# Group norm factors of the first three batches formed for 88 partitions by 6 numbers and spread over the channels through DRAM

## The chip, the core and the metric

The kernel runs on one core of one Trainium2 chip. The metric is the device time of one execution in microseconds, lower is better; the time of a kernel is the median of its runs. TensorE (PE) multiplies matrices into PSUM, VectorE (DVE), ScalarE (ACT) and GpSimd (POOL) work on tiles in SBUF and PSUM, SyncE (SP) issues most of the DMA transfers. Each engine takes its instructions in the order in which they were put at compile time and waits where one isn't ready.

## What is computed

One layer of a decoder for a prompt of 256 tokens and 8 sampled tokens (264 columns in all): a gated feed-forward network, a mixer that runs 16 attention heads beside 16 heads of an RWKV-7 recurrence, an output projection, and a second feed-forward network. The change lies in the group norm behind the recurrence. For every head (64 channels) and every token the 64 values are normalised:

```python
    S, y = wkv_scan(wkv0, r, logw, k, v, kk, a)
    mean = jnp.mean(y, axis=-1, keepdims=True)
    var = jnp.mean((y - mean) ** 2, axis=-1, keepdims=True)
    yn = ((y - mean) * lax.rsqrt(var + GN_EPS)).reshape(B, T, RWKV_WIDTH) * ln_w.astype(f32) + ln_b.astype(f32)
    bonus = jnp.sum(r * k * r_k.astype(f32), axis=-1, keepdims=True) * v
    out = (yn + bonus.reshape(B, T, RWKV_WIDTH)) * g
```

## The kernel before

Activations lie with channels on the 128 partitions and the 264 tokens along the columns, so a pair of heads fills one tile of 128 x 264. The 16 RWKV heads are eight such pairs, worked on in four batches of two pairs.

The bulk of the time is `gemm` (line 135): weights stream from DRAM in chunks of 128 x 512 (`chunk`, line 123). SP loads a chunk into `raw` (6 buffers), ACT rounds it to `hi`, DVE takes the rest `lo` = `raw` - `hi` (4 buffers each), and PE runs twelve matmuls of 264 columns per chunk: `hi` twice, `lo` once for each of four 128 x 128 blocks. Two feed-forward networks stand around the mixer. In the mixer the input projection (`win`, 38 tiles of four chunks) and the output projection (`wout`) run as the steady stream, and the recurrence, the attention and the norm are generators ("tasks") that `tick` moves on by one step after each chunk; `pause(n)` lets a task sleep for n ticks. What the program writes in this order is then put into a fixed order on each engine by a scheduler that works with a model of the chip. So an edit in one task can move the instructions of others.

A batch goes through `prep` (gates, decay, key norm) and `chain`: a triangular solve on DVE (60 small instructions on the tiles `X`, `Xt`, `st`, ending in `PT`), a row of small PE steps (`PT`x`gm`, `TT`x`W`, `kr`x`TT`, ...) with copies on ACT and DVE between them, the states `S`, the output `y`, and last `gnorm` for each of the two pairs. `gnorm` (line 707) runs in float32 on PE: one product of `y` with a 128 x 128 matrix `cm` takes the mean away, ACT squares the result into `r`, one product with `bo` (ones within each head) sums the squares over a head's 64 channels and puts the sum on all 64 partitions, ACT takes the root, DVE the reciprocal of 128 x 264 numbers, and DVE multiplies. Behind it lines 694 and 695 apply weight, bias and gate. The product with `cm` stays in its PSUM bank (`m`, 5 buffers) until the last multiplication.

DMA transfers of the mixer go through SP too: `sa`, which carries the solve's input through DRAM to a layout with another partition order, the loads `ld` (6 buffers), the residual `x` from `xsp`. ACT issues a few output transfers, one of them `out_sh` (line 887), which waits for a copy that POOL makes.

Of the kernel before, what the change touches and what calls it, by code (L numbers as in the profile page):

```python
# [7 lines left out]
F32 = mybir.dt.float32  # L8
F32R = mybir.dt.float32r
AF = mybir.ActivationFunctionType  # L10
ALU = mybir.AluOpType
AX = mybir.AxisListType

P = 128
NP = 256
NB = 8
T = NP + NB
# [7 lines left out]
HALF = (slice(0, 64), slice(64, 128))  # L25
# [5 lines left out]
ROW = 320  # L31
NWARM = 11
NGM, NKR, NUV, NTT, NBT = 10, 5, 3, 2, 5
NSTEP = 4
DWAIT = (11, 11, 11, 3)
PW = (2, 1, 3, 2, 9)
# [1 line left out]
LKV = 26  # L38
SEQ = [('b', 0), ('b', 1), ('b', 2), ('b', 3), ('kv', 0), ('kv', 1), ('kv', 2), ('kv', 3), ('q', 0), ('q', 1), ('q', 2), ('q', 3), ('q', 4), ('q', 5), ('q', 6), ('q', 7)]
PASS = [[0,1,2,3],[4,5,6,7],[8,9,10,11,12,13,14,15]]  # L40

VG1, VGM, VG2, VGF = 0, 16, 32, 48
VMU, VKK, VKA, VA0, VRK, VLW, VLB, VSK, VSD = 64, 90, 98, 106, 114, 122, 130, 138, 154
NVEC = 155
# [3 lines left out]
def body(tc, I, O):  # L48
    nc = tc.nc
    V, A, G, TE, SP = nc.vector, nc.scalar, nc.gpsimd, nc.tensor, nc.sync  # L50
# [3 lines left out]
    def uid(s):  # L54
        cnt[0] += 1
        return f"{s}{cnt[0]}"

    def tt(e, out, a, b, op):
        return e.tensor_tensor(out=out, in0=a, in1=b, op=op)  # L59
# [8 lines left out]
    def act(out, in_, f, **k):  # L68
        return A.activation(out=out, in_=in_, func=f, **k)  # L69

    def bc(ap, shape):
        return ap.broadcast_to(list(shape))

    def mm(out, lhsT, rhs, start=True, stop=True, **k):
        return TE.matmul(out, lhsT, rhs, start=start, stop=stop, **k)  # L75

    def behind(i):
        tc.add_manual_dep(i.ins, big[0].ins.name, mybir.DependencyInfo(mybir.DependencyClass.NoSync, mybir.DependencyReason.SCHED_ONLY))
        return i
# [16 lines left out]
    def pause(n):  # L96
        for _ in range(n):
            yield

    with ExitStack() as ctx:  # L100
# [4 lines left out]
        dp = ctx.enter_context(tc.tile_pool(name="dp", bufs=1, space=bass.MemoryType.DRAM))  # L105
# [16 lines left out]
        def mp():  # L122
            return pp.tile([P, 512], F32, tag="m", bufs=NM, name=uid("m"))
# [33 lines left out]
        eps = cp.tile([P, 2], F32, name="eps")  # L157
# [199 lines left out]
        def mixing_body(mx, n2, n3, XD, XR):  # L357
# [3 lines left out]
            def ring(shape, tag, bufs):  # L361
                return mx.tile(list(shape), F32, tag=tag, bufs=bufs, name=uid(tag))
# [6 lines left out]
            ident, bo, cm = C[:, CID:CID + P], C[:, CBO:CBO + P], C[:, CCM:CCM + P]  # L369
# [50 lines left out]
            class Batch:  # L420
                pass

            def c4(x):
                return x[:, :NP].rearrange("p (c t) -> p c t", c=4)

# [127 lines left out]
            def chain(bt):  # L553
                n = bt.n
# [31 lines left out]
                for h in range(2):  # L586
                    x = h * 64
                    V.transpose(TT[x:x + 32, :, 0:32], TN[x:x + 32])
                yield from pause(7)
                ps = mp()  # L590
                for k in range(n):
                    for c in range(4):
# [14 lines left out]
                for h in range(2):  # L607
                    r = slice(h * 64, h * 64 + 32)
                    A.copy(TT[r, :, 32:64], ps[r, :n * P].rearrange("p (c t) -> p c t", t=32))
                yield  # L610
                Ys = [yb[bt.p0 + k] for k in range(n)]
                uv = bt.UV
                N = ring((P, n, 4, 64), "N", 1)
# [9 lines left out]
                for k in range(n):  # L623
                    v = wus[k].rearrange("p (c t) -> p c t", c=4)
                    for h in range(2):
                        (V.tensor_copy, A.copy)[h](uv[HALF[h], :, k, HALF[h]], v[HALF[h], :, 64:128])
                yield
                pbs = [mp() for _ in range(n)]
                for k in range(n):
                    for c in range(1, 4):  # L630
# [51 lines left out]
                    A.dma_start(O["wkvp"][bt.p0 + k], S[:, k])  # L682
                g2s = [load(I["g2"][bt.p0 + k], (P, P)) for k in range(n)]
                gps = []
                gs = [gnorm(Ys[k]) for k in range(n)]
                for _ in range(PW[3] + 1):
                    for g in gs:
                        next(g)
                    yield
# [14 lines left out]
                        A.copy(XR[HALF[h], 4], xt[0:64, HALF[h]])  # L704
                yield

            def gnorm(y):
                yp = mp()
                mm(yp[:, :T], cm, y)
                r = tmp()  # L710
                act(r, yp[:, :T], AF.Square)
                yield from pause(PW[3])
                vp = mp()
                mm(vp[:, :T], bo, r)
                act(r, vp[:, :T], AF.Sqrt, scale=1.0 / 64, bias=eps[:, 1:2])
                V.reciprocal(r, r)
                tt(V, y, yp[:, :T], r, ALU.mult)
                yield
# [395 lines left out]
```

## Time and profile before

| | |
|---|---|
| median of 3 runs | 1958.44 us (1957.58 to 1960.91) |
| the profiled execution: its own time | 1958.83 us |
| its span, first to last instruction | 1957.0 us |
| granted TensorE clock | 0.998 |
| PE busy | 1940.1 us |
| DVE busy | 1313.1 us |
| ACT busy | 1036.4 us |
| first and last product of `y` with `cm` | 904.7 and 1087.9 us |

The first feed-forward network runs up to about 780 us, the mixer from there to about 1200 us, the second network behind it. In the profile's rows a float32 matmul of the program appears as two records, each with a weight load of its own; a matmul of the gemm (float32r) is one record. Records overlap, so a mean duration is longer than the step from one to the next.

### The profile page before, as it was taken

What the parts mean: (1) busy time and instruction counts of PE and PEld (TensorE: products, weight loads), DVE (VectorE), ACT (ScalarE), POOL (GpSimd) and SP (SyncE); (2) the same over time, 40 slices, a digit from 0 to 9 for tenths busy, and PEclk for the clock granted to TensorE, in tenths of its full rate; (3) what the DMA queues carried; (4) which work ended last, traced back from release to release, by engine and by line L of the source; (5) the groups of instructions that cost most, each with busy time, mean ns of one, the idle gap of its engine ahead of it and who ended that gap; (6) DMA issues with size and microseconds to landing.
All of it is one profiled execution on the core that took longest, in us unless ns stands there. A gap on an engine that the chain in (4) does not pass through costs nothing.

```text
span 1957.0 us, 45229 instructions
## 1 busy us (share of the span) xinstructions
PE 1940.1 (99%) x17011; PEld 1922.1 (98%) x17011; DVE 1313.1 (67%) x2591; ACT 1036.4 (53%) x2069; POOL 264.1 (13%) x382
## 2 busy tenths in 40 slices
PE   9999999999999999999999999999999999999998
PEld 9999999999999999999889999999999999999998
DVE  5865555655556567799988766766666666666665
ACT  5644444444444456665556755654444444444445
POOL 0401001010010122232210000210101001010012
PEclk9999999999999999999999999999999999999999
DMA  7666666666656567555455455566666666666654
GB/s 241 178 194 194 186 194 196 184 189 178 188 183 185 184 194 230 165 162 153 136 151 167 137 157 185 176 187 188 191 189 193 188 194 191 191 195 183 195 182 148
DMA packets 218875, 357.26 MB, mean 183 GB/s; under 512 B 33552, under 2 KB 72352, under 8 KB 218656
## 3 DMA queue, kind: packets, MB, share of 16 engines
q1 hardware_dynamic: 212144, 345.76, 59.4%
q10 hardware_dynamic: 6512, 8.61, 1.4%
q8 instruction: 133, 2.18, 0.4%
q14 instruction: 86, 0.70, 0.1%
HBM read 346.67 MB, written 9.69 MB: 182 GB/s over the span
## 4 chain that ended last, share of the span: by engine, by line
PE 95%; DVE 3%; DMA 1%; issue 1%; ACT 1%; SPq 0%; DVEq 0%; POOL 0%; ACTq 0%
PE acc L75 87%; PE m L75 7%; DVE lo L59 1%; DVE Xt L59 0%; DVE st L59 0%; DMA Xt<-sa 0%; DMA x<-in_x 0%; DMA raw<-in_win 0%; DVE y L59 0%; SPq L564 0%; DVE gm L59 0%; ACT t L69 0%; DMA sa<-gm 0%; PE m L782 0%; ACT BT L521 0%
## 5 line engine op out<-in xcount | busy, mean ns | idle before, releaser
L59 DVE TENSOR_TENSOR lo<-raw,hi 128x512 fp32r<-128x512 f32 (+1 forms) x1288 | 874.5, 683 | 511.0 <-ACT hi L132 489.8
L132 ACT CAST hi<-raw 128x512 fp32r<-128x512 f32 (+1 forms) x1288 | 777.0, 606 | 822.0 <-PE acc L75 741.5
L75 PE MATMUL acc<-x,hi 128*128 128x264 f32 x5034 | 932.7, 286 | 2.2 <-DVE o L62 1.2
L75 PEld LDWEIGHTS acc<-x,hi 128*128 128x128 f32 x5034 | 781.4, 189 | 5.8 <-ACT hi L132 2.4
L75 PE MATMUL acc<-x,lo 128*128 128x264 f32 x2517 | 719.8, 286 | 0.5 <-DVE lo L59 0.5
L75 PE MATMUL acc<-h,hi 128*128 128x264 f32 x2752 | 495.0, 284 | 0.0
L75 PEld LDWEIGHTS acc<-x,lo 128*128 128x128 f32 x2517 | 475.5, 189 | 2.9 <-DVE lo L59 1.3
L75 PEld LDWEIGHTS acc<-h,hi 128*128 128x128 f32 x2752 | 424.4, 189 | 0.0
L75 PE MATMUL acc<-h,lo 128*128 128x264 f32 x1376 | 387.8, 284 | 0.0
L75 PEld LDWEIGHTS acc<-h,lo 128*128 128x128 f32 x1376 | 259.2, 189 | 0.0
L59 POOL TENSOR_TENSOR t<-t,t 128x264 f32<-128x264 f32 x74 | 80.3, 1085 | 1095.9 <-DVE t L59 949.7
L75 PE MATMUL acc<-y,hi 128*128 128x264 f32 x648 | 122.7, 284 | 0.0
L75 PE MATMUL acc<-o,hi 128*128 128x264 f32 x648 | 120.1, 284 | 0.0
L75 PE MATMUL acc<-kv,hi 128*128 128x264 f32 x582 | 109.2, 284 | 0.0
L75 PEld LDWEIGHTS acc<-y,hi 128*128 128x128 f32 x648 | 101.2, 189 | 0.1
L75 PEld LDWEIGHTS acc<-o,hi 128*128 128x128 f32 x648 | 100.1, 189 | 0.0
L62 DVE SCALAR_TENSOR_TENSOR x<-acc,x 128x264 f32<-128x264 f32 x192 | 81.2, 427 | 24.5 <-PE acc L75 23.6
L75 PE MATMUL acc<-y,lo 128*128 128x264 f32 x324 | 92.0, 284 | 0.0
L75 PE MATMUL acc<-o,lo 128*128 128x264 f32 x324 | 92.0, 284 | 0.0
L75 PEld LDWEIGHTS acc<-kv,hi 128*128 128x128 f32 x582 | 90.0, 189 | 0.0
L59 DVE TENSOR_TENSOR t<-acc,t 128x264 f32<-128x264 f32 x156 | 67.4, 432 | 32.8 <-PE acc L75 32.8
L75 PE MATMUL acc<-kv,lo 128*128 128x264 f32 x291 | 82.7, 284 | 0.0
(280 smaller groups left out, 1534.9 us busy)
## 6 DMA issues: line engine op xcount, KB each, us to landing
raw<-in_gu SPq DMA_DIRECT2D x688, 256.0 KB, 3.4
raw<-in_dn SPq DMA_DIRECT2D x224, 256.0 KB, 2.9
raw<-in_win SPq DMA_DIRECT2D x152, 256.0 KB, 3.4
raw<-in_dn SPq DMA_DIRECT2D x160, 192.0 KB, 2.7
raw<-in_wout SPq DMA_DIRECT2D x64, 256.0 KB, 3.3
xsp<-x ACTq DMA_DIRECT2D x16, 132.0 KB, 3.6
x<-xsp SPq DMA_DIRECT2D x16, 132.0 KB, 4.0
ld<-in_sT SPq DMA_DIRECT2D x16, 128.0 KB, 3.7
```

The lines of the kernel that those rows point to most:

```text
L59: return e.tensor_tensor(out=out, in0=a, in1=b, op=op)
L62: return V.scalar_tensor_tensor(out=out, in0=a, scalar=s, in1=b, op0=op0, op1=op1)
L75: return TE.matmul(out, lhsT, rhs, start=start, stop=stop, **k)
L132: A.copy(hi[:, :w], raw[:, :w])
```

## The change

For batches 0, 1 and 2 (`SMALL = (1, 1, 1, 0)`) the product with `bo` gives way to `sums`: for j = 0, 1, 2 the squares of every third token (88 columns) are the stationary operand and two columns of `bo`, one per head, the moving one. The result is 88 partitions x 6 numbers, one sum of squares for each head and token. Root and reciprocal are taken of these 6 columns. `spread` writes them to DRAM as two rows of 264 and, two ticks later, loads each row into the 64 partitions of its head, into the tile `r`; three ticks later DVE multiplies. The centred `y` is copied from PSUM to SBUF by ACT right behind the square. The generator of such a batch gets five more ticks. Batch 3 keeps the former way. `LAG`, `P1` and `P2` replace constants by names with the same values.

```diff
+LAG = (7, 7, 7, 7)
+P1 = 1
+P2 = 1
+SMALL = (1, 1, 1, 0)
+HOP = (2, 3)
...
+            def sums(sq):
+                sm = mp()
+                for j in range(3):
+                    mm(sm[0:88, j * 2:j * 2 + 2], sq[:, j:T:3], bo[:, 0:P:64])
+                return sm[0:88, 0:6].rearrange("p (j h) -> p h j", h=2)
+
+            def spread(s, to):
+                d = dp.tile([2, T], F32, tag=uid("dr"), name=uid("dr"))
+                SP.dma_start(d.rearrange("h (p j) -> p h j", j=3), s)
+                yield from pause(HOP[0])
+                for h in range(2):
+                    behind(SP.dma_start(to[HALF[h]], bc(d[h:h + 1], (64, T))))
+                yield from pause(HOP[1])
...
-                gs = [gnorm(Ys[k]) for k in range(n)]
-                for _ in range(PW[3] + 1):
+                gs = [gnorm(Ys[k], SMALL[bt.i]) for k in range(n)]
+                for _ in range(PW[3] + 1 + SMALL[bt.i] * sum(HOP)):
...
-            def gnorm(y):
+            def gnorm(y, small):
                 yp = mp()
                 mm(yp[:, :T], cm, y)
                 r = tmp()
                 act(r, yp[:, :T], AF.Square)
+                if small:
+                    A.copy(y, yp[:, :T])
+                    yield from pause(PW[3])
+                    s = ring((88, 2, 3), "s", 4)
+                    act(s, sums(r), AF.Sqrt, scale=1.0 / 64, bias=eps[0:88, 1:2])
+                    V.reciprocal(s, s)
+                    yield from spread(s, r)
+                    tt(V, y, y, r, ALU.mult)
+                    yield
+                    return
                 yield from pause(PW[3])
```

The scheduler moves much else with it, from the first norm (904.7 us) on. Three places in the order of the instructions follow. In a row, the left name is what is written, and numbers behind names are buffers.

DVE, the norm of batch 0, before (`t_12822` and `t_12826` are the two pairs' roots, `lo` the gemm's weights, `Xt` and `st` the solve of batch 1):

```order
L716 RECIPROCAL t_12822<-t_12822 128x264
L59 TENSOR_TENSOR st_13013<-X_12413,Xt_12414 128x72
L716 RECIPROCAL t_12826<-t_12826 128x264
L59 TENSOR_TENSOR lo_13221<-raw_13219,hi_13220 128x512
L59 TENSOR_TENSOR y_112<-m_12820,t_12822 128x264
L59 TENSOR_TENSOR Xt_12414<-Xt_12414,st_13013 128x4x18
L59 TENSOR_TENSOR lo_13267<-raw_13265,hi_13266 128x512
L59 TENSOR_TENSOR y_112<-m_12824,t_12826 128x264
```

and now:

```order
L735 RECIPROCAL s_12866<-s_12866 88x6
L63 TENSOR_TENSOR Xt_12414<-Xt_12414,st_12998 128x3x19
L63 TENSOR_TENSOR st_13019<-X_12413,Xt_12414 128x72
L735 RECIPROCAL s_12875<-s_12875 88x6
L63 TENSOR_TENSOR Xt_12414<-Xt_12414,st_13019 128x4x18
L63 TENSOR_TENSOR st_13022<-X_12413,Xt_12414 128x68
L63 TENSOR_TENSOR Xt_12414<-Xt_12414,st_13022 128x4x17
L63 TENSOR_TENSOR st_13025<-X_12413,Xt_12414 128x64
L63 TENSOR_TENSOR Xt_12414<-Xt_12414,st_13025 128x4x16
L462 TENSOR_SCALAR t_13035<-keep,t_12962 128x256
L63 TENSOR_TENSOR st_13028<-X_12413,Xt_12414 128x60
L63 TENSOR_TENSOR lo_13237<-raw_13235,hi_13236 128x512
```

The first multiplication of `y` stands six rows further on, behind another `lo`, and with it a wait for DMA. From the first of these reciprocals to the end of batch 1's solve (`PT`) DVE has 85 instructions with 17 `lo` before, 81 with 14 `lo` now; on PE, from batch 0's sums of squares to the first product with that `PT`, 218 matmuls of the gemm stand before, 167 now, and the other matmuls between are the same but for the sums.

SP at the same place before (`raw` are the gemm's weights, `ld` the mixer's loads):

```order
L131 DMA raw_13479<-in_win 128x512
L366 DMA ld_13297<-in_sT 128x256
L366 DMA ld_13464<-in_lw 128x256
L131 DMA raw_13516<-in_win 128x512
L131 DMA raw_13564<-in_win 128x512
```

and now:

```order
L135 DMA raw_13495<-in_win 128x512
L435 DMA dr_12873<-s_12866 88x2x3
L435 DMA dr_12882<-s_12875 88x2x3
L370 DMA ld_13313<-in_sT 128x256
L438 DMA t_12822<-dr_12873 64x264 x2
L438 DMA t_12827<-dr_12882 64x264
L135 DMA raw_13532<-in_win 128x512
L438 DMA t_12827<-dr_12882 64x264
L135 DMA raw_13580<-in_win 128x512
```

Two stores and three of the four loads stand ahead of the next weights. Counted along each engine's order, 620 chunks of the gemm stand on PE ahead of batch 0's sums, 630 on SP ahead of the first store, and 624 `lo` on DVE ahead of its first small reciprocal.

ACT, batch 1's chain, before (`TT` at line 609 is waited for by PE, `hi` are the gemm's weights):

```order
L600 COPY W_13184<-m_13497 32x256 x2
L132 COPY hi_14036<-raw_14035 128x512
L132 COPY hi_14077<-raw_14076 128x512
L887 DMA out_sh<-shc 128x234
L609 COPY TT_12420<-m_13534 32x8x32 x2
L132 COPY hi_14118<-raw_14117 128x512
L132 COPY hi_14172<-raw_14171 128x512
L622 COPY W_13184<-m_13583 128x192
```

and now, first around `TT`, then where `out_sh` stands, with nine rows left out between the two:

```order
L136 COPY hi_13942<-raw_13941 128x512
L627 COPY TT_12420<-m_13550 32x8x32 x2
L136 COPY hi_13979<-raw_13978 128x512
L136 COPY hi_14028<-raw_14027 128x512
L640 COPY W_13200<-m_13599 128x192
```

```order
L658 COPY PT_13201<-m_13655 128x192
L495 COPY uv_12919<-m_13732 64x2x64 x4
L136 COPY hi_14099<-raw_14098 128x512
L915 DMA out_sh<-shc 128x234
L136 COPY hi_14142<-raw_14141 128x512
```

The output transfer no longer stands ahead of `TT`; it is now behind `W`, `uv` and `PT` of the same batch.

More of the change, by code (lines that the diff above doesn't have):

```diff
@@ L588, in chain @@
                     V.transpose(TT[x:x + 32, :, 0:32], TN[x:x + 32])
-                yield from pause(7)
+                yield from pause(LAG[bt.i])
                 ps = mp()
@@ L609, in chain @@
                     A.copy(TT[r, :, 32:64], ps[r, :n * P].rearrange("p (c t) -> p c t", t=32))
-                yield
+                yield from pause(P1)
                 Ys = [yb[bt.p0 + k] for k in range(n)]
@@ L626, in chain @@
                         (V.tensor_copy, A.copy)[h](uv[HALF[h], :, k, HALF[h]], v[HALF[h], :, 64:128])
-                yield
+                yield from pause(P2)
                 pbs = [mp() for _ in range(n)]
```

## The prediction

> **What bounds the kernel now.** I read the page's first two parts, then the chain of waits, then who PE waited for in the stretch that the change reaches.
>
> ```profile
> PE 1940.1 (99%) x17011; PEld 1922.1 (98%) x17011; DVE 1313.1 (67%) x2591; ACT 1036.4 (53%) x2069; POOL 264.1 (13%) x382
> DVE  5865555655556567799988766766666666666665
> PE 95%; DVE 3%; DMA 1%; issue 1%; ACT 1%; SPq 0%; DVEq 0%; POOL 0%; ACTq 0%
> ```
>
> PE is busy 99% of the span and makes 95% of the chain that ended last. Time can go only where PE does less work or stands less. DVE is close to full only in the slices of the mixer (7 to 9 tenths), where the change lies. The product of `y` with `cm`, up to which both kernels have the same order on PE, is at 904.7 us; from just behind it to the end of the chains (1110 us) PE waited for:
>
> ```profile
> PE m L75 <- ACT TT L609: 1.5, 1, 1.5
> PE m L75 <- DVE W L622: 1.3, 2, 0.9
> PE acc L75 <- DVE o L62: 1.2, 1, 1.2
> PE m L701 <- ACT XR L703: 0.4, 1, 0.4
> PE m L732 <- ACT XD L536: 0.3, 1, 0.3
> PE acc L75 <- DVE lo L59: 0.3, 1, 0.3
> PE acc L75 <- DVE x L59: 0.2, 1, 0.2
> ```
>
> Columns: total us, times, longest. That is 5.2 us in all, and the most that a lighter DVE or ACT can give back.
>
> **PE's own work: nearly nothing.** Six matmuls with `bo` go, six times three with 88 x 2 results come.
>
> ```profile
> 904.87 1.05 PE L75 MATMUL m<-y,C 128*128 128x264 f32 x4
> 905.88 0.40 PE L75 MATMUL acc<-x,hi 128*128 128x264 f32 x2
> ...
> 1946.13 0.63 PE L75 MATMUL m<-ones,sq 128*88 128x1 f32 x6 [0.65 <-ACT sq L69]
> 1946.62 0.80 PE L75 MATMUL m<-sq,ones 128*128 128x128 f32 x5
> ...
> 920.77 11.81 PE acc L75 x98
> ```
>
> The last row gives a gemm matmul 11.81 / 98 = 0.12 us. Two float32 matmuls of 264 columns (four records from 904.87 on) and one gemm matmul lie ahead of 905.88, so one costs (1.01 - 0.12) / 2 = 0.45 us. The final norm at the kernel's end already forms sums in the new shape with one column: six records (three matmuls) from 1946.13 to 1946.62, 0.49 us. So 6 x (0.49 - 0.45) = +0.2 us. New is that every third column is loaded as weights; no row has that. Bounds: the smallest float32 records, and the whole duration of a weight load as if none overlapped:
>
> ```profile
> L75 PE MATMUL m<-XD,ld 64*64 64x2 f32 x256 | 8.6, 195 | 0.0
> L75 PEld LDWEIGHTS acc<-x,hi 128*128 128x128 f32 x5034 | 781.4, 189 | 5.8 <-ACT hi L132 2.4
> ```
>
> 8.6 / 256 = 0.034 us a record gives 6 x (0.20 - 0.45) = -1.5 us; 0.189 us gives 6 x (1.13 - 0.45) = +4.1 us. I take +0.2, since the final norm's matmul is the same but for the step and one column.
>
> **DVE's relief.** The large reciprocals are the dearest single instructions there:
>
> ```profile
> L716 DVE RECIPROCAL t<-t 128x264 f32<-128x264 f32 x6 | 10.7, 1798 | 1.9 <-ACT t L69 1.9
> L753 DVE RECIPROCAL stb<-stb 128x4 f32<-128x4 f32 x8 | 1.3, 169 | 0.1
> 991.68 1.80 DVE L442 RECIPROCAL t<-m 128x264 f32<-128x264 f32 x1
> 995.33 0.39 DVE L62 SCALAR_TENSOR_TENSOR o<-acc,rs 128x264 f32<-128x264 f32 x1
> 995.98 0.67 DVE L59 TENSOR_TENSOR lo<-raw,hi 128x512 fp32r<-128x512 f32 x1
> 995.86 0.36 PE L75 MATMUL acc<-x,hi 128*128 128x264 f32 x1 [1.24 <-DVE o L62]
> ```
>
> The first row's six (batches 0 to 2) shrink to the second row's size: 10.7 - 6 x 0.17 = 9.7 us of DVE, 3.2 per batch. The other rows show what a late DVE costs: a reciprocal of 1.8 us and a backlog behind it let `o` empty its bank late, and PE stands 1.2 us. In the new order batch 1's large reciprocals (3.6 us) no longer stand ahead of this, so I count the 1.2 as gone, and `W`'s 1.3 too: it waits for a copy in the same backlog. The early copy of `y` also frees a PSUM bank sooner; no wait for a bank `m` is among PE's rows, so that is worth nothing here. Multiplying from SBUF rather than from PSUM I cost at nothing: DVE's rows of 264 columns take 0.42 to 0.43 us from either.
>
> **ACT.** One stall has another cause:
>
> ```profile
> 953.03 0.68 POOL L412 COPY shc<-pj 128x9 f32<-128x9 f32 x1 [4.38 <-DVE pj L59]
> 953.75 0.35 ACTq L887 DMA_DIRECT2D out_sh<-shc  x1
> 954.14 0.75 ACT L609 COPY TT<-m 32x256 f32<-32x256 f32 x2 [3.83 <-POOL shc L412]
> 954.55 0.71 PE L75 MATMUL m<-kr,TT 64*64 64x128 f32 x4 [1.46 <-ACT TT L609]
> ```
>
> `out_sh` stands on ACT ahead of `TT` and waits for POOL, POOL for DVE; `TT` is behind it, and PE loses 1.5 us. In the new order `TT` comes first, and the 1.5 us go. ACT's roots get shorter, but six copies come:
>
> ```profile
> 908.11 1.28 ACT L69 ACT_TABLE_LOAD   x1
> 909.40 0.85 ACT L69 ACTIVATE t<-m,eps 128x264 f32<-128x264 f32 x2
> 910.21 0.62 ACT L132 CAST hi<-raw 128x512 fp32r<-128x512 f32 x1
> 913.61 0.39 ACT L69 ACTIVATE t<-m 128x264 f32<-128x264 f32 x1
> 909.90:943.97 34.07, 34.07 (x362) 32.97 (x361) 33.03 (x85) 22.93 (x59) 8.53 (x17) 1.00 0.57 158
> ```
>
> (Last row: length, then busy us of PE, weight loads, DVE, ACT, POOL, then clock, DMA share and GB/s.) A copy of 264 columns is costed like the last activation, 0.39 us, two per batch 0.8. ACT is idle 11.1 of the 34 us between batch 0's norm and batch 1's solve, which covers them; without that cover they would delay `hi` by 0.8 us.
>
> **The way through DRAM.** Rows for a store, a load behind it, and a load of the same size (KB, us to landing):
>
> ```profile
> sa<-gm SPq DMA_DIRECT2D x32, 16.0 KB, 1.7
> Xt<-sa SPq DMA_DIRECT2D x16, 32.0 KB, 2.9
> ld<-in_g SPq DMA_DIRECT2D x8, 64.0 KB, 3.1
> x<-xsp SPq DMA_DIRECT2D x16, 132.0 KB, 4.0
> raw<-in_win SPq DMA_DIRECT2D x152, 256.0 KB, 3.4
> ```
>
> From the small reciprocal to `r` in SBUF: 1.7 for the store, 0.4 for issuing the second half's load, 3.1 to land, 5.2 us. DVE's first multiplication waits for it, and the `lo` behind that. What covers it is what stands on ACT behind the roots: a table load (1.28), three operations of 264 columns (0.39 to 0.5), a `hi` (0.62) that DVE's next `lo` waits for, and two more operations (0.4 each) that two DVE operations behind that `lo` wait for; those two (0.42 each), a small one (0.2) and a second `lo` (0.67) come before the multiplication. That is 5.8 us, an estimate from these rows and the order, and hides the hop with 0.6 us to spare. At the long end, 4.0 (the `xsp` row) for store and load each, it is 8.4 us, 2.6 late. I charge 0.4 per batch, 1.2 us, nearer to the medians: the stores' 12-byte pieces are smaller than those of `sa`.
>
> The Trainium skill, "DMA: Bandwidth & Descriptors", section "Specifications", says that pieces below 512 bytes are written by read-modify-write, which speaks against this store. The trace's 128-byte pieces (`sa`) landed in 1.7 us, sooner than any larger row above; no run here shows 12 bytes. By the row the sum below stays; by the rule, for which the page gives no price, the store comes nearer to the long end and the sum nearer to the second rival's.
>
> On SP six stores and twelve loads, and their waits, stand ahead of weights. At batch 0 SP is ten chunks ahead of PE, 10 x 12 x 0.12 = 14 us; the stop (1.7 us and six issues of 0.4) takes 4.1, landing, cast and `lo` 3.4 + 0.6 + 0.7. The total of 8.8 is inside 14.
>
> **The tightest place** is batch 1's solve:
>
> ```profile
> 943.97 0.42 DVE L59 TENSOR_TENSOR PT<-X,unit 128x256 f32<-128x256 f32 x1
> 945.52 0.69 PE L75 MATMUL m<-PT,gm 32*32 32x32 f32 x32
> ```
>
> By the window row above, DVE is 97% busy over its 85 instructions from the large reciprocals to `PT` and ends `PT` at 944.39, 1.1 us before PE takes it. In the new order PE gets there 218 - 167 = 51 gemm matmuls sooner, 6.1 us. DVE's list is shorter by two large reciprocals (3.6), three `lo` (3 x 0.67) and two small ones, longer by the two new reciprocals: 5.6 us. That leaves 1.1 - 0.5 = 0.6 us. A late hop comes through here undamped.
>
> **Sum**, against the profiled execution's 1958.83: -1.5 (`TT`) -1.2 (`o`) -1.3 (`W`) +0.2 (PE) +1.2 (hop) = -2.6. That execution lies 0.4 above the median of 1958.44, so I forecast 1955.9. What a measurement of this kernel can tell from no change is about 0.2%, 3.9 us: faster means below 1954.5, slower above 1962.4, and the forecast lies between. Its own range is 1954.3 to 1960.
>
> **Rivals.** One more row, DVE's waits for data that come back from DRAM:
>
> ```profile
> DVE st L59 <- DMA Xt<-sa: 2.9, 2, 1.7
> ```
>
> *The hop is fully hidden and all waits go:* -5.2 + 0.2 gives 1953.4, with the weights at the lower bound 1951.7. For it: SP's lead, and DVE's backlog shrinks by 9.7 us. Against: the four smallest waits (1.2 us) aren't behind the norm's instructions, and the scheduler has moved PE up to where it waits again. *The hop lands late:* at 8.4 us DVE stands 2.6 us at a multiplication, `lo` and `PT` come late, and PE stands 2.6 less 0.6. With both multiplications of a batch late, two batches cost 2 x 2 x 2.0 = 8.0 and three 12.0 in place of 1.2: 1958.4 - 4.0 + 0.2 + 8.0 = 1962.6, or 1966.6; I take the middle, 1964.6. It decides from a hop of 5.8 us. For it: DVE already waited twice for `Xt`, in all 2.9 us. Against: the medians above. *The waits only move:* PE meets other waits of the same sum, 1958.6; for it: PE's order is set by a model in both kernels, and any order leaves a few us.
>
> **How the numbers follow.** Forecast 0.40, all waits gone 0.28, hop late 0.20, waits moved 0.12. All waits gone lies below 1954.5 in nearly all of it, and the forecast in a tenth: faster 0.30. The late hop lies above 1962.4: slower 0.20. The rest, 0.50, is the same. The range of 1951.7 to 1965 leaves out the dearer half of the late hop.
>
> **What would show it.** Right: `L735 RECIPROCAL s` near 0.18 us; a record of the 88 x 2 matmuls near 0.08 us; `t<-dr` landing within 5.8 us of the reciprocal; no wait of PE for `TT` behind `out_sh`, none for `o` near batch 1's norm; PE's waits from 905 to 1110 us near 2.4 us. Wrong: PE waiting for `PT` or for `lo` behind `y<-y,t`, DVE waiting for DMA `t<-dr` over 1 us a time, or records of 0.15 us and more.

## The result, and the profile after

The changed kernel takes 1963.44 us (median of 20 runs, 1960.95 to 1968.14), the kernel before 1959.19 us (20 runs, 1957.55 to 1962.73). The ratio is 1.0021 with a 95% interval of 1.0014 to 1.0028: slower, and the whole interval lies above 1. The forecast was 1955.9 us and no change. Of all the runs in this document one, of the experiment e9, was slow (3199.35 us at a clock of 0.555), and its ratio leaves it out. The profiled execution took 1962.78 us, 3.95 more than the one before.

From the first two parts of the changed kernel's page and its chain of waits:

```profile
PE 1943.8 (99%) x17035; PEld 1925.5 (98%) x17035; DVE 1308.1 (67%) x2591; ACT 1036.9 (53%) x2075; POOL 267.7 (14%) x382
...
PE 94%; DVE 3%; DMA 2%; ACT 1%; issue 0%; SPq 0%; DVEq 0%; POOL 0%; ACTq 0%
```

PE is busy 3.7 us more. DVE is busy 5.0 us less, and nobody has gained by it. On the chain DMA stands at 2% where it had 1%. The waits of PE from 905 to 1110 us (total, times, longest):

```profile
PE acc L79 <- DVE lo L63: 2.4, 3, 0.9
PE m L79 <- DVE W L640: 1.7, 1, 1.7
PE m L810 <- ACT XR L722: 0.7, 1, 0.7
PE m L79 <- DVE t L63: 0.6, 1, 0.6
PE m L719 <- ACT XR L721: 0.5, 1, 0.5
PE m L79 <- ACT TT L627: 0.2, 1, 0.2
```

That is 6.1 us for 5.2 before. The wait for `TT` is down to 0.2 and the one for `o` is gone, as forecast, but three waits for `lo` have come, one in each changed batch, and `W` costs more than it did. The longest of DVE's waits for DMA, over the whole execution:

```profile
DVE y L63 <- DMA t<-dr: 8.0, 3, 3.8
...
DVE st L63 <- DMA Xt<-sa: 3.9, 1, 3.9
```

The first row did not exist before: three times DVE stood at a product with the spread factors, 8.0 us in all. How one such wait reaches PE is in the chain of waits of the changed kernel, batch 0 (start, length, what):

```profile
909.74 0.19 DVE s L735
...
909.96 4.22 DMA dr<-s
...
914.25 0.50 SPq L438
914.76 0.05 issue
914.81 2.85 DMA t<-dr
...
917.75 0.12 DVE y L63
917.88 0.23 issue
918.11 0.22 DVE Xt L63
918.33 0.60 DVE lo L63
...
922.27 0.69 DVE lo L63
922.96 0.04 issue
923.00 1.12 PE acc L79 x7
```

From the small reciprocal's end (909.93) to the product (917.75) the way through DRAM, the hop, takes 7.8 us: 4.2 for the store, 0.5 for issuing a load, 2.9 for the load behind it. In the other two batches it takes 8.5 and 9.3. DVE had run out of other work 2.3 us before, and the `lo` that the gemm needs stands behind the product:

```profile
914.76 0.69 DVE L63 TENSOR_TENSOR lo<-raw,hi 128x512 fp32r<-128x512 f32 x1
917.75 0.43 DVE L63 TENSOR_TENSOR y<-y,t 128x264 f32<-128x264 f32 x1 [2.31 <-DMA t<-dr]
...
923.00 0.39 PE L79 MATMUL acc<-x,lo 128*128 128x264 f32 x1 [0.87 <-DVE lo L63]
```

(The first two rows are DVE's timeline, the third is PE's.) From one matmul's start to the next the three `lo` waits cost 1.04, 1.05 and 0.82 us beyond a gemm step, 2.9 us; the view of waits counts less, since it works with modelled ends.

The other part of the loss is PE's own. In PE's timeline of the changed kernel the sums of batch 0 run from 908.40 to 909.75:

```profile
908.40 1.49 PE L79 MATMUL m<-C,t 128*88 128x2 f32 x12
909.75 0.69 PE L79 MATMUL m<-tw,ld 65*128 65x264 f32 x2
```

Twelve records in 1.35 us, mostly 120 ns from start to start. Three batches take 4.05 us, where the six products with `bo` took 6 x 0.45 = 2.7: +1.35 us.

### The profile page after: what moved, and what is told of

It is laid out like the page before. It is cut to its first block, busy times and chain, and to the rows that moved or that the text cites. A ratio compares the mean times of both kernels' runs of the same rounds, so it can differ in the third digit from the quotient of the medians.

```text
span 1961.0 us, 45330 instructions
## 1 busy us (share of the span) xinstructions
PE 1943.8 (99%) x17035; PEld 1925.5 (98%) x17035; DVE 1308.1 (67%) x2591; ACT 1036.9 (53%) x2075; POOL 267.7 (14%) x382
## 4 chain that ended last, share of the span: by engine, by line
PE 94%; DVE 3%; DMA 2%; ACT 1%; issue 0%; SPq 0%; DVEq 0%; POOL 0%; ACTq 0%
PE acc L79 86%; PE m L79 7%; DVE lo L63 1%; DMA dr<-s 0%; DVE Xt L63 0%; DVE st L63 0%; DMA t<-dr 0%; DMA sa<-gm 0%; DVE y L63 0%; DMA x<-in_x 0%; ACT hi L136 0%; PE m L810 0%; DMA ld<-in_kc 0%; DVE gm L63 0%; DMA Xt<-sa 0%
```

## The experiments

Two measures stand beside the median. *Wait for factors* is DVE's wait for DMA at the product, in us. *Stretch* is the time in the profiled execution from a gemm matmul that all orders have at 904 us to the 1598th gemm matmul behind it, where all have left the mixer; it leaves out what other stages do. *Half clock* is the part of the stretch, in us, in which the trace's clock record grants TensorE half its clock. Each ratio is to the kernel before on the same chip, whose median stands in the column *before*. The chips differ in it by up to 1.6 us, so medians of runs with different *before* are compared by their ratios.

| run | wait for factors | PE's waits 905 to 1110 | stretch | half clock | median | before | ratio, 95% |
|---|---|---|---|---|---|---|---|
| before | | 5.2 | 295.99 | 0 | 1959.19 | | |
| changed | 8.0 | 6.1 | 299.75 | 3.4 | 1963.44 | 1959.19 | 1.0014 to 1.0028 |
| e1 | 8.1 | 6.6 | 300.53 | 6.8 | 1963.28 | 1960.13 | 1.0004 to 1.0021 |
| e2 | 6.5 | 5.1 | 298.21 | 3.4 | 1961.38 | 1960.13 | 0.9997 to 1.0014 |
| e3 | 1.3 | 6.7 | 300.22 | 3.4 | 1964.29 | 1960.13 | 1.0010 to 1.0027 |
| e4 | none | 4.2 | 298.02 | 6.8 | 1961.81 | 1960.13 | 1.0004 to 1.0021 |
| e5 | none | 4.8 | 297.05 | 3.4 | 1962.30 | 1960.17 | 0.9999 to 1.0017 |
| e6 | none | 6.1 | 297.15 | 6.8 | 1960.49 | 1960.17 | 0.9994 to 1.0012 |
| e7 | 8.8 | 7.5 | 302.45 | 3.4 | 1965.97 | 1960.17 | 1.0021 to 1.0049 |
| e8 | none | 5.3 | 300.15 | 10.2 | 1961.53 | 1960.17 | 0.9999 to 1.0016 |
| e9 | 2.2 | 1.7 | 293.47 | 3.4 | 1959.20 | 1960.56 | 0.9982 to 1.0000 |
| e10 | none | 5.6 | 297.31 | 6.8 | 1960.21 | 1960.56 | 0.9986 to 1.0003 |
| e11 | none | 6.0 | 297.85 | 3.4 | 1960.50 | 1960.56 | 0.9988 to 1.0005 |
| e12 | none | 4.9 | 297.67 | 6.8 | 1961.02 | 1960.56 | 0.9987 to 1.0004 |
| e13 | 6.1 | 5.3 | 297.25 | 0 | 1960.65 | 1960.77 | 0.9996 to 1.0013 |
| e14 | 7.0 | 6.2 | 299.69 | 6.8 | 1962.83 | 1960.77 | 1.0003 to 1.0020 |
| e15 | 5.0 | 4.0 | 297.54 | 6.8 | 1959.93 | 1960.77 | 0.9986 to 1.0003 |
| e16 | 6.6 | 8.0 | 304.28 | 10.2 | 1968.71 | 1960.77 | 1.0029 to 1.0056 |
| e17 | 3.4 | 6.2 | 300.31 | 13.7 | 1960.56 | 1959.88 | 0.9994 to 1.0012 |

At half clock a gemm matmul takes 0.22 us for 0.12 (in the changed kernel from 1071.17 to 1074.58 us). The pieces last 3.41 us or a multiple of it, so each 3.41 us cost up to 1.6 us, an estimate: 3.41 x (1 - 0.12 / 0.22). The profiled kernel before has none in its stretch and the changed one has one, so up to 1.6 of the 3.8 us between their stretches are the clock's. Some pieces begin at a wait of PE (e11 waits 2.28 us for `W`, and the clock halves at 961.47), others among small matmuls without one (1071.17 in the changed kernel); what brings them on was not tried. Executions of one kernel differ in it: 49 runs of the kernel before with a recorded clock of 0.998 have a median of 1959.4 us, 22 with 0.995 one of 1962.8. The medians and ratios are of many executions, a stretch is of one.

Landings below are from the issue's start to the last semaphore event of that transfer in the trace.

### What the sums cost (e1, e5)

```diff
-                    mm(sm[0:88, j * 2:j * 2 + 2], sq[:, j:T:3], bo[:, 0:P:64])
+                    mm(sm[0:88, j * 2:j * 2 + 2], sq[:, j * 88:j * 88 + 88], bo[:, 0:P:64])
```

> The sums take 88 tokens that lie side by side as weights in place of every third one; the three sums of a batch's half then belong to other tokens than the store assumes, so the factors go to other tokens than the reference's. The order on every engine stays that of the changed kernel. Weight theory: the 120 ns between the 36 records of these sums come from the stride of the loaded columns. Expected: about 78 ns a record as in the final norm, 36 x 0.042 = 1.5 us less, last matmul at about 1951.0 us after 1952.5, median near 1961.9. Rival (the size of the result or the changing bank sets the step): still 120 ns, last matmul at 1952.5, median 1963.4.

The weight loads of the sums, first in the changed kernel, then in this one (groups by line and form: busy us, mean ns of one):

```profile
L79 PEld LDWEIGHTS m<-C,t 128*88 128x88 f32 x36 | 4.6, 206 | 0.0
```

```profile
L79 PEld LDWEIGHTS m<-C,t 128*88 128x88 f32 x36 | 3.2, 158 | 0.0
```

And PE's timeline of this run, batch 0:

```profile
908.64 1.03 PE L79 MATMUL m<-C,t 128*88 128x2 f32 x12
909.53 0.69 PE L79 MATMUL m<-tw,ld 65*128 65x264 f32 x2
```

A load of every third column takes 206 ns, one of neighbouring columns 158, and the twelve records go from 1.35 to 0.89 us (909.53 - 908.64): 1.4 us less over three batches. The time followed at most in part. PE came earlier to the first two `lo` waits and stood there 1.53 and 1.65 us beyond a step, for 1.04 and 1.05: what it waited for there was set by the factors' landing and not by PE, and the first two batches' savings were gone behind these waits. The stretch came out 0.8 us longer, but with one more piece at half clock, worth up to 1.6. The ratio is 0.08% lower (1.6 us) with overlapping intervals. So the half of the expectation on the records held; on the time, this run leaves it open.

The same edit without the way through DRAM (the edit of e4 with the one above):

> As the run without the hop, with the sums' weights taken as 88 neighbouring tokens; the order on every engine is that of the run without the hop, and the outputs are not the reference's (y multiplied by its squares). Time from the product of y with cm in batch 0 to the same gemm matmul far behind the mixer is 295.99 us in the kernel before, 299.75 in the changed one, 298.02 without the hop. Theory (what is left without the hop is PE's own work: strided sums 1.62 us, waits 0.4): the records fall from 120 to 78 ns, 1.4 us go and nothing takes them back, as no late factor stands behind them: 296.6, last matmul near 1949.5, median near 1960.3. Rival (waits take back whatever PE saves, as in the run with neighbouring tokens and the hop): 298 to 299.

With the same order as e4, PE is 0.94 us ahead of it at a gemm matmul at 973 us, 0.47 for each of the first two batches. So up to there the saving comes back in full, where no late factor stands behind it. Behind that the two executions differ in the clock, and the stretch falls by 0.97 us with 3.4 us at half clock less. The median didn't fall (1962.30 after 1961.81), and the two intervals overlap: the time of this part isn't settled by medians.

### What the way through DRAM costs (e2, e3, e4, e7, e8)

```diff
-                    behind(SP.dma_start(to[HALF[h]], bc(d[h:h + 1], (64, T))))
+                    behind(SP.dma_start(to[HALF[h]], bc(I["win"][0][h:h + 1, 0:T], (64, T))))
```

> The factors are still stored to DRAM, but the loads that spread them take rows of a weight matrix in their place and so wait for no store; the outputs are not the reference's. Hop theory: DVE's waits for the spread factors (8.0 us in three places) come from the store's landing, and the three waits of PE for lo behind them (about 1.0 us each beyond a step) with them. Expected: DVE's waits for the loads under 2 us in all, the three lo waits gone, last matmul 2.5 to 3 us earlier (about 1949.7), median near 1960.6. Rival (waits only move): PE meets other waits of about the same sum, last matmul within 0.8 us of 1952.5.

The stretch fell by 1.5 us, half of what was expected; the ratio fell by 0.16%, 3.1 us, as much as was expected, though the intervals just touch. DVE still waited 6.5 us. The loads no longer wait for the store, and SP issued three of them right behind it, from 911.52 us on, but they landed only after 5.9 to 6.1 us, where the changed kernel's of this batch took 2.9 to 3.5. The same loads of a weight row that this order puts ahead of a store landed after 2.6 to 3.1 us. Such a store holds up what is issued behind it, wait or no wait.

```diff
+HOP = (2, 12)
...
-                    tt(V, y, y, r, ALU.mult)
+                    behind(tt(V, y, y, r, ALU.mult))
```

> The hop stays as it is, with the right result, but the product with the spread factors is put some 10 to 16 DVE instructions later (the second pause 12 ticks, and the product ordered behind the gemm matmul issued then). Hop theory: DVE no longer stands for the factors, the lo waits go: 2 to 3 us less, last matmul near 1950, median near 1960.9, unless the later norm is missed somewhere. Rival (waits only move): no gain, last matmul within 0.8 us of 1952.5 or later.

DVE's wait went to 1.3 us and the `lo` waits to 0.5, as the hop theory has it, but the time didn't fall: the later product moved other instructions, and PE now waited 2.5 us for a load `ld`, 1.6 for `TT` and, at line 719, 1.5 for an activation. Moving the product elsewhere in the order exchanges one wait for others.

```diff
-                    yield from spread(s, r)
+                    yield from pause(sum(HOP))
```

> No store and no load: y is multiplied by the squares that lie in the buffer already, the reciprocal of 88 x 6 numbers is formed and not used; pauses as before. The outputs are not the reference's. Hop theory: DVE never waits for the factors, and SP issues 18 DMAs fewer: last matmul 3 us earlier or better (about 1949.5, with the 120 ns records left), median near 1960.4. Rival (SP's queue is what counts, by late weights): the gain is above that of the run without the store's wait by over 1 us. Rival (waits only move): within 0.8 us of 1952.5.

The ratio is 0.08% (1.6 us) below the changed kernel's, with overlapping intervals, and the stretch 1.7 us, with 6.8 us at half clock for 3.4. The three `lo` waits are gone but for 0.6, and another wait stands in their place:

```profile
PE m L79 <- ACT TT L627: 2.9, 1, 2.9
PE m L79 <- DVE PT L63: 0.7, 1, 0.7
PE acc L79 <- DVE lo L63: 0.6, 1, 0.6
```

Without the transfers the scheduler puts another order on every engine, so this run takes away the hop and changes the order too. It was no clean test.

```diff
-                SP.dma_start(d.rearrange("h (p j) -> p h j", j=3), s)
+                A.dma_start(d.rearrange("h (p j) -> p h j", j=3), s)
```

> The two stores of the 12-byte pieces are issued by ACT and not by SP, with the right result: loads issued behind them on SP no longer stand in the same queue. If a store of 12-byte pieces holds up its whole queue (a ld issued 0.5 us behind it landed after 4.9 us; with no wait for the store the spread loads behind it still took 5.9 us): the lds near it land in 3 to 3.7 us, and the store itself keeps its 4 us, so the spread is hardly earlier: stretch within 0.7 us of the changed kernel's 299.75. If the store is slow only because of what is ahead of it in SP's queue: it lands in under 2.5 us, DVE's wait for the factors falls from 8.0 to under 4 us, stretch near 298.3.

The `ld` behind the store, now on another engine's queue, still landed after 4.6 us (4.9 in the changed kernel), and the store, issued at 910.17, held the loads back to 914.26: the slowness isn't that of one queue. This fits the Trainium skill, "DMA: Bandwidth & Descriptors", section "Issuing engines are not separate DMA queues": transfers run on the same sixteen engines whoever issues them. The run is the slowest with three changed batches: the wait for factors is 8.8 us, and PE waits 2.0 us for `TT` again. Both forks of the expectation missed the time.

In e8 the store stays and only the loads go:

```diff
-                for h in range(2):
-                    behind(SP.dma_start(to[HALF[h]], bc(d[h:h + 1], (64, T))))
...
```

> The stores are made, nothing is loaded back and y is multiplied by the squares in the buffer (outputs not the reference's). Theory (the store costs only through the product that waits for it): as without the hop, 298.0. Rival (the store's 4 us on SP's queue delay weights and Xt by themselves): 298.7 or more, and DVE's wait for Xt from DRAM above the 5.5 us of the run without the hop.

The median (1961.53) is near that of e4 (1961.81), and so is the ratio. The profiled execution had 10.2 us at half clock, and its stretch isn't to be compared with e4's. So a store that nobody waits for costs nothing that the medians show.

### The store's pieces (e9)

```diff
-                SP.dma_start(d.rearrange("h (p j) -> p h j", j=3), s)
+                SP.dma_start(d.rearrange("h (q x) -> (h q) x", x=6), s.rearrange("p h j -> p (h j)"))
```

> The changed kernel with each store written as 88 pieces of 24 bytes in place of 176 of 12, so that the factors land in another sequence than they are read (outputs not the reference's); loads and their wait for the store stay. If a store's time goes by the number of its pieces: landing 2.0 to 2.6 us after 3.9 to 4.9, DVE's wait for the factors from 8.0 to about 3 us, PE's lo waits from 2.4 to about 1, stretch from 299.75 to about 298.5, median 1.2 us below the changed kernel's 1963.4. If a floor sets it whatever the pieces: landing still near 4, stretch 299.5 to 300.

This is the run that decides. The stores landed after 2.0 to 2.7 us, where the changed kernel's took 3.8 to 4.9. SP's timeline, the changed kernel first, then this one: the loads `t<-dr` are issued as soon as the store has landed.

```profile
909.96 0.79 SPq L435 DMA_DIRECT2D dr<-s  x2
910.92 0.37 SPq L370 DMA_DIRECT2D ld<-in_sT  x1
914.25 2.45 SPq L438 DMA_DIRECT2D t<-dr  x3
```

```profile
910.18 0.78 SPq L435 DMA_DIRECT2D dr<-s  x2
911.14 0.37 SPq L370 DMA_DIRECT2D ld<-in_sT  x1
912.35 1.78 SPq L438 DMA_DIRECT2D t<-dr  x3
```

4.3 us from store to load there, 2.2 here. The product then finds its factors ready in DVE's timeline (no bracket behind the row):

```profile
915.60 0.43 DVE L63 TENSOR_TENSOR y<-y,t 128x264 f32<-128x264 f32 x1
```

PE's waits from 905 to 1110 us are these two:

```profile
PE m L79 <- DVE W L640: 1.3, 1, 1.3
PE acc L79 <- ACT hi L136: 0.4, 1, 0.4
```

1.7 us of PE's waits for 6.1, and a stretch 6.3 us below the changed kernel's, with as much half clock. By the ratios the two kernels are 0.30% apart, 5.9 us, with about 2 us of doubt either way. Eleven of the runs lie between 1955.16 and 1961.34 us; the profiled one took 1956.74, one of the shortest. The strided sums are still in, and the form of the store, the number and size of its pieces and the places where they land, is all that was edited. The order on PE is the changed kernel's up to 1002 us, and on DVE and SP up to 1039; behind that some dozens of rows of DVE and ACT and some hundreds of PE's records stand elsewhere. In this common part, without half clock in either, PE gains 3.4 us, above all because two `lo` waits and the one for `PT` are gone. So these 3.4 us are the hop's and not those of another order.

### DVE's relief and the wait for `TT` alone (e6, e10, e11, e12)

These are edits of the kernel before.

```diff
...
-                V.reciprocal(r, r)
+                few = r[0:88, 0:6] if less else r
+                V.reciprocal(few, few)
```

> The kernel before, with the reciprocals of batches 0 to 2 cut to 88 x 6 numbers (the rest of each buffer keeps its roots, so the outputs are not the reference's): DVE gets the 9.7 us of relief, and nothing else of the change is made. The forecast's terms (waits for TT, o and W gone with the relief): 4.0 us less than before, stretch of 295.99 near 292, median near 1955.5. Rival (a lighter DVE meets other waits, above all its own for Xt from DRAM; PE's waits only move): stretch 295 to 297, median within 1 us of the kernel before.

Nothing came of it: 1960.49 us, where the kernel before has 1960.17 on the same chip. The stretch is 1.2 us longer, with 6.8 us at half clock. PE's waits from 905 to 1110 us:

```profile
PE m L75 <- DVE W L622: 3.3, 1, 3.3
PE m L75 <- DVE y L59: 1.1, 1, 1.1
PE acc L75 <- DVE o L62: 0.9, 1, 0.9
PE m L75 <- ACT t L69: 0.8, 1, 0.8
```

DVE's timeline ahead of the largest of them, for `W`:

```profile
1012.43 0.68 DVE L59 TENSOR_TENSOR lo<-raw,hi 128x512 fp32r<-128x512 f32 x1
...
1013.76 0.20 DVE L59 TENSOR_TENSOR st<-X,Xt 128x57 f32<-128x57 f32 x1
1013.99 0.22 DVE L59 TENSOR_TENSOR Xt<-Xt,st 128x57 f32<-128x57 f32 x1
1014.13 0.35 DVE L622 COPY W<-m 128x192 f32<-128x192 f32 x1
```

DVE doesn't stand idle there. Ahead of `W` lie `lo` and steps `st` and `Xt` of another batch's solve: in the order that the scheduler made for the lighter DVE, `W` stands behind that work.

> A second form of DVE's relief in the kernel before: the six large reciprocals become copies in place of 264 columns (about 0.4 us for 1.8, so 8.4 us less DVE; y is multiplied by roots, the outputs are not the reference's). The scheduler puts another order on the engines than in the first form, which tells luck of one order from worth of the relief. If relief is worth what the forecast's terms say (4.0 us): median near 1956. If it is worth nothing in this stage (first form: stretch 297.15, time equal to before): within 1.5 us of the kernel before.

A copy in place of the reciprocal gives 1960.21 us and a stretch of 297.31: no gain a second time. PE's largest wait is again `W`, 2.8 us, and the two forms pass most of the same gemm matmuls within 0.3 us of each other, so the second confirms the first more than it varies it.

```diff
-                        A.dma_start(O["sh"], shc)
+                        G.dma_start(O["sh"], shc)
```

> The kernel before with one edit: out_sh is issued by POOL, behind the copy that it waits for, and no longer by ACT ahead of TT. The order on PE, DVE and SP is that of before. If TT's wait is worth its own time: PE's wait of 1.5 us for TT goes to under 0.3, stretch 295.99 to about 294.5, median 1.5 us less. If DVE's or Xt's lateness then ends another wait (waits move): the stretch falls by under 0.5 us.

Here the order on PE, DVE and SP is untouched. `TT` no longer waits, and the largest of PE's waits are:

```profile
PE m L75 <- DVE W L622: 3.3, 2, 2.3
PE acc L75 <- DVE o L62: 1.2, 1, 1.2
PE acc L75 <- DVE lo L59: 0.6, 2, 0.4
```

`W` was 1.3 us and is 3.3: behind `TT` on the same chain of small steps comes a copy on DVE, and there PE now waits 2.3 us for 0.4. With SP as the issuer the same happens:

> As the run with out_sh on POOL, but issued by SP, which waits for POOL's copy with weights queued behind it. If SP's lead covers it: as on POOL, 294.5. If not: weights come late, PE waits for lo, 296 or more.

At the same place PE waits 2.3 us for `W` again. SP's lead covers the wait. Both medians are those of the kernel before, within intervals that would still hold a gain of 1.5 us. In the profiles `TT`'s 1.5 us were worth nothing by themselves: the wait for `W` behind it took 1.9 back, and a piece at half clock came on top.

### Forms with the right result (e13 to e17)

e13 keeps the 24-byte pieces in the sequence in which they are stored. The load takes the whole row, and the product picks its three of every six:

```diff
...
+                    w = ring((P, 2 * T), "w", 2)
+                    yield from spread(s, w)
+                    v = y.rearrange("q (p j) -> q p j", j=3)
+                    tt(V, v, v, w.rearrange("q (p x) -> q p x", x=6)[:, :, 0:3], ALU.mult)
```

> The stores of 24-byte pieces with the right result: each half's load takes the whole row of 88 x 6 numbers from its own offset on (2.1 KB a partition, 131 KB, after 66 KB), and the product picks three numbers of every six. Hop theory: the store lands after 2.0 to 2.7 us, the load 0.3 to 0.8 us later than the short one, the stretch is 293.5 to 295, under the 295.99 before; median 1959 to 1960.3, at or just below the kernel before. If the gain was luck of one order: stretch 298 or more, median near 1962.

The stores landed after 2.2 to 3.1 us, the loads, now of twice the bytes, after 2.9 to 5.4. The wait for factors came back to 6.1 us, and with it the stretch to 297.25. The ratio is 0.17% (3.3 us) below the changed kernel's, and the median is that of the kernel before.

> As the run before, with the right result and 88 neighbouring tokens as weights of the sums (and the product reading the factors in that sequence). Weight theory: the records fall from 120 to 78 ns, and with no late factor behind them 1.4 us come back in full: stretch 1.4 less than with strided columns (near 292.6), median 1.4 us less (near 1958.3), faster than the kernel before. Rival (waits take it back): no difference to the strided run.

Slower than e13 by 2.2 us in the medians, against the expectation, though the intervals overlap. The product of e13, then of e14 (busy us, mean ns, idle before):

```profile
L63 DVE TENSOR_TENSOR y<-y,w 128x264 f32<-128x264 f32 x6 | 2.5, 424 | 6.1 <-DMA w<-dr 6.1
```

```profile
L63 DVE TENSOR_TENSOR y<-y,w 128x264 f32<-128x264 f32 x6 | 3.8, 633 | 7.0 <-DMA w<-dr 7.0
```

Read with a step of six numbers the product takes 633 ns for 424. That is 0.2 us each time just ahead of `lo`, and PE, earlier by its cheaper sums, waited 4.6 us for `lo` for 2.7. Whether this is the reason was not tried; of the 2.4 us between the two stretches all can be the clock's (6.8 us at half clock for none).

> The run with 24-byte pieces and the short loads (factors to wrong places) with neighbouring tokens as weights; the order on every engine is that of the strided run, whose stretch was 293.47. Weight theory: 292.1, median 1.4 us below 1959.2. Rival (waits take it back): 293.5.

The stores took up to 3.2 us in this execution and the wait for factors was 5.0 us, not 2.2; the stretch is 297.54, with 6.8 us at half clock for e9's 3.4, and the ratio 0.9994 for 0.9991. Once more PE's saving didn't show where factors were late. The pair shows the hop's price in one and the same order too: in batch 0 the stores took 3.2 and 3.1 us for 2.1 and 2.7, and PE stood 0.65 us beyond a step at `lo` and 0.86 at `PT`, two waits that e9 doesn't have.

e16 is e14 with `SMALL = (1, 1, 1, 1)`:

> As the right run with neighbouring tokens, with the last batch's norm in the small form too. The last batch has no later batch's solve to fill its hop, and the gemms of the next stage wait for its y: if the hop stands on the path there, the stretch is 1 to 3 us longer than with three batches; if gemm matmuls of other tiles fill it, 0.5 us shorter.

The median is 5.9 us above e14's and the stretch 4.6 longer, more than expected. That the last batch's hop itself stands on the path isn't shown. DVE waits 0.6 us there for the factors, while PE, behind it, waits 1.9 us for a load `ld<-in_kc` and then has 6.8 us at half clock.

In e17 DVE transposes the factors of both pairs of a batch in blocks of 32 x 32, so that 32 neighbouring tokens make one piece:

```diff
...
+                V.reciprocal(s[0:88, 0:12], s[0:88, 0:12])
+                V.transpose(f, s)
+                d = dp.tile([2, 2 * T], F32, tag=uid("dr"), name=uid("dr"))
+                for b, n in ((0, 32), (1, 32), (2, 24)):
+                    x = b * 32
+                    SP.dma_start(d.rearrange("h (c q) -> (h c) q", q=88)[:, x:x + n], f[x:x + 12, 0:n])
```

> The change in another form, with the right result: sums over 88 neighbouring tokens, both pairs of a batch in one tile of 88 x 12 numbers, one sqrt and one reciprocal, a 32 x 32 transposition on DVE, three stores of 12 pieces of 96 to 128 bytes in place of two of 176 of 12 bytes, and one load per half (2.1 KB a partition) for both pairs. If the landing of the store goes by its pieces: 1.5 to 2.2 us each (as for sa), the factors are there 5.5 to 6 us after the reciprocal, DVE waits under 3 us for them in all, the stretch is 292 to 294 (forecast's mechanism with a hop inside its cover, and sums 1.4 us cheaper), median 1957.5 to 1959.5, below both kernels. Rival (the load of 2.1 KB pieces or the three issues eat it, or another wait appears): DVE waits 5 us and more, stretch 296 to 298, median 1960 to 1962.

The stores landed after 1.5 to 2.1 us in two batches, 3.2 to 3.6 in the third; DVE waited 3.4 us for factors. The ratio is 0.18% (3.5 us) below the changed kernel's, and the median is that of the kernel before, no better. The profiled execution had 13.7 us at half clock, so its stretch says little, and one wait of DVE in it was 6.6 us for `Xt`, which comes from DRAM too. So no form with the right result beat the kernel before; e13 and e17 reach it.

## Why the prediction was wrong

**The way through DRAM** is the step that failed: "From the small reciprocal to `r` in SBUF: 1.7 for the store, 0.4 for issuing the second half's load, 3.1 to land, 5.2 us." It took 4.2 + 0.5 + 2.9 = 7.8 us with gaps. Issue and load were right; the store's price was that of 128-byte pieces (`sa`), and 176 pieces of 12 bytes took 3.8 to 4.9. The cover was estimated well: 5.8 us in the prediction, 5.5 measured (DVE ran dry at 914.76 + 0.69 = 915.45). So the second rival came, at a hop near its 8.4 us and at 1963.4 for its 1964.6; its chance of 0.20 was too low. That its time came so close is in part luck: it charged 8 to 12 us for PE's waits behind the hop, where the profile shows 3.8 (2.9 at `lo`, 0.9 at `PT`), and took off 4.0 for the other waits, of which 2.1 went. The page that the prediction weighed, the Trainium skill, "DMA: Bandwidth & Descriptors", section "Specifications", spoke for that rival, and the trace agrees as far as pieces of 12 bytes landed late. It doesn't show the limit of 512 bytes: pieces of 24 and of 128 bytes are below it too and landed in 2.0 to 2.7 us (e9) and 1.7 (`sa`, the median). I went by the row of larger pieces instead. e9 shows the price: 5.9 us by the ratios, 6.3 in the profiled executions, 3.4 of them before the orders part, where the sum charged 1.2.

**PE's own work** was mis-sized: +1.35 us measured (+1.62 in the expectations, which counted to the next gemm matmul), +0.2 forecast. "I take +0.2, since the final norm's matmul is the same but for the step and one column": the step was the price. With neighbouring columns (e1) the sums take 3 x 0.89 = 2.67 us, as much as the products with `bo`, so a second column costs nothing that the records show. The upper bound of +4.1 held. The Trainium skill, "SBUF — State Buffer", section "Door 1: The DMA port swizzle (why `[64,N]` ≈ `[32,N]`)", says that float32 may be read with steps up to four numbers at no loss. For these weight loads the trace differs: 206 ns with a step of three, 158 without.

**`TT` and `o`** went as forecast, 1.5 to 0.2 and 1.2 to nothing. **`W`** did not: 1.3 before, 1.7 after, in batch 2. What failed with them is the rule of the sum that each wait is worth its own length. e11 and e12 took `TT`'s wait away alone, and the one for `W` behind it grew from 0.4 to 2.3; e6 and e10 took the reciprocals alone, and PE's waits stayed at 6.1 and 5.6. Yet in e9, where the change is whole and the hop in time, PE's waits are 1.7 us, even below the 2.4 that the prediction gave, and the stretch is 2.5 us shorter than before, with the strided sums. That is one execution, and a short one; the ratio of 0.9982 to 1.0000 puts the gain at the edge of what the runs can tell. If it is real, relief and order pay there together, while the relief alone did not. Whether it is the earlier copy of `y`, the shorter ACT work or the place of the norm in that order that would make the difference was not tried.

**The tightest place** was named rightly, and that "a late hop comes through here undamped". The forecast left 0.6 us of margin at batch 1's `PT`; with the hop late PE stood there 0.59 us. From PE's timeline of the changed kernel, with DVE's row of `PT` ahead of it:

```profile
941.53 0.43 DVE L63 TENSOR_TENSOR PT<-X,unit 128x256 f32<-128x256 f32 x1
...
942.09 0.69 PE L79 MATMUL m<-PT,gm 32*32 32x32 f32 x32 [0.59 <-DVE t L63]
```

(`PT` ends at 941.96, next to PE's start; the `t` that the view names is a small operation behind it.)

**SP's lead** was right: in the changed kernel no `lo` of the mixer waits for its `raw`. The small reciprocals were right as well, 0.18 us each.

## What to carry to other kernels

Price a store by its pieces: the same 2.1 KB landed in 3.8 to 4.9 us as 176 pieces of 12 bytes (3.0 to 5.0 in other runs with this store, once 1.7) and in 2.0 to 3.2 as 88 of 24, and whoever waits for the data pays the difference. Whether the number or the size of the pieces sets the time, no run here separates. If no row of the trace has a piece that small, a trip through DRAM belongs at the long end of its bounds, above all where its cover is within a microsecond of it. And waits that stand on one chain of small steps aren't to be added up as gains: take one away alone first, and look at which one grows. Before two profiled executions are compared, their clock is: one piece of 3.41 us at half clock is worth as much as many of the waits here.

## What was not expected of the hardware

A store of 12-byte pieces delays transfers issued after it, on its own queue (an `ld` 4.9 us, 3.0 in e9; loads without a wait 5.9 to 6.1) and on another engine's (4.6). Weights with a step of three columns load in 206 ns for 158, and the records go 120 ns apart for 78. A DVE product whose second operand is read with a step of six numbers takes 633 ns for 424. Inside the mixer the granted clock falls to half for pieces of 3.41 us, none to four of them in a stretch, in executions whose mean clock is 0.995 to 0.998.
